# Second output projection: residual rows and two tiles' residuals beside the last attention units, two weight blocks split into the smaller pool

## The chip, the cores and the metric

The kernel runs on one core of a Trainium2 chip. The metric is the device time of one execution in microseconds (us), lower is better; before the change the median of 3 runs is 1395.11 us. Five engines work side by side, each on its own instruction stream, and synchronise by semaphores: TensorE (PE) multiplies matrices, VectorE (DVE), ScalarE (ACT) and GpSimd (POOL) do the elementwise work, and SyncE (SP) issues transfers. Data lies in the on-chip SBUF; matmuls write to PSUM, in banks of 128 partitions by 512 floats.

## The reference

Two encoder layers on 1024 tokens of 1024 channels in float32. Layer A is a dilated sliding-window attention, layer B a latent attention with 16 heads. The change touches only the end of layer B: the output projection `y @ w_out`, and the residual and LayerNorm behind it.

```python
def mixer_mla(u, w_in, q_norm, w_uq, kv_norm, w_ukv, w_out):
    ...
    o = o.transpose(1, 0, 2, 3, 4).reshape(B, S, WIDTH_B)
    y = o * jax.nn.silu(gate)
    return y @ w_out

def reference(...):
    for i in range(DEPTH):
        mod = jax.nn.silu(c) @ ada_w[i] + ada_b[i]
        shift, scale, gate = jnp.split(mod[:, None, :], 3, axis=-1)
        u = x * (1 + scale) + shift
        ...
        x = layernorm(DEEPNORM_ALPHA * x + gate * y, ln_g[i], ln_b[i])
    return x
```

## The kernel before

**Arithmetic.** A float32 product is made of three: each operand is split into a rounded high part and the rest, and high times high, high times low and low times high are added up (`mm3`, lines L89, L90 and L91, one 512-column matmul each). So each weight block and each block of activations needs a high copy (ACT) and a low part, which is source minus high copy (DVE or POOL).

**Attention of layer B** runs over 128 units u, a unit being 128 queries of one head; units stand in pairs w, 64 in all. Four steps of different units are interleaved: scores, softmax, the transposes of the weights (`pth` high and `ptl` low, L1270 to L1274), and for each pair the product with the values (`back(w)`, PE line L1293). `back` ends with `osum`: two copies on ACT (L1298, L1299), a multiply on DVE (L1302), and on POOL a sum (L1305) and the multiply with the gate (L1306) into `gT`, the input of the output projection: 8 blocks of 128 channels. The last pairs, 62 and 63, fill the last tokens of block 7.

**The output projection** works on 8 tiles of 128 tokens, in PSUM tiles `po` of which two exist at a time. Each tile adds up 8 weight blocks times two halves times three products: 48 matmuls. Block b of `wo_b` is loaded (`woraw`, SP), and split by `b_wo_split` into `wh`, `wl` (L101, L102); `b_yt(b, hf)` splits `gT` of block b for one half of the tokens into `ytb` (L1363 on ACT, L1364 on DVE). Half 0 serves tiles 0 to 3, half 1 tiles 4 to 7. Blocks 0 to 3 of tiles 0 and 1 are multiplied beside the last attention units (u = 128 and 129 in the loop), the rest in `layer_b_out`: blocks 4 to 7 of tile 0, then of tile 1, then whole tiles.

**The end of a tile.** The residual tile `x` is loaded from DRAM (L1395) and multiplied by a row and added to another on POOL (L1396, L1397); both rows have been multiplied by ALPHA on ACT (L1390). `finish(i)` multiplies `po` with the gate row (`zb`, L1402), which is the last reader of that PSUM tile; adds the residual (L1403); and after a `yield`, one tile later, does mean, variance and scaling (L1404 to L1410) and stores.

**What sets the order.** PE and SP execute in the order in which the program emits (`manual_schedule(engines=FIXED)`). On DVE, ACT and POOL a scheduler orders the instructions when the program is built. Buffers come from two pools of 128 x 1024 float32 tiles: G with 33 (`gt`) and H with 14 (`ht`); whoever asks for a tile of a full pool waits until an old one has had its last reader.

Of the kernel before, what the change touches and what calls it, by code (L numbers as in the profile page):

```python
# [15 lines left out]
F32 = mybir.dt.float32  # L16
F32R = mybir.dt.float32r
AF = mybir.ActivationFunctionType
ALU = mybir.AluOpType
# [10 lines left out]
ALPHA = math.sqrt(2.0)  # L30
# [11 lines left out]
def f32(ap):  # L42
    return ap.bitcast(F32)
# [23 lines left out]
class Trunk:  # L67
# [1164 lines left out]
    def layer_b_attention(self):  # L1232
        nc = self.nc
        st = {}

        def front(u):
            hd, t = u // 8, u % 8
            q, k = self.q[hd], self.kb[hd % 3]
            s = self.PB.tile([P, 1024], F32, tag="s", bufs=2, name=self.nm("s"))
            ts = slice(t * P, t * P + P)  # L1240
            for j in range(2):
                ks = slice(j * 512, j * 512 + 512)
                self.mm3(s[:, ks], q[0][:, ts], q[1][:, ts], k[0][:, ks], k[1][:, ks], True, True)
            if t == 7:
                self.q.pop(hd)
            st[u] = s

        def soft(u):
            s = st[u]
            m = self.M.tile([P, 4], F32, tag="mb", bufs=4, name=self.nm("mb"))  # L1250
            nc.vector.tensor_reduce(m[:, 0:1], s, axis=AX.X, op=ALU.max, negate=True)  # L1251
            st[u] = (s, m)

        def expo(u):
            s, m = st[u]
            pr = self.ht(F32, "pr")
            nc.scalar.activation(pr, s, AF.Exp, bias=m[:, 0:1], accum_out=m[:, 1:2])  # L1257
            st[u] = (pr, m)

        def middle(u):  # L1260
            pr, m = st.pop(u)
            a = u % 2
            if a == 0:
                st["pt"] = [(self.gt(F32R, "pth"), self.gt(F32R, "ptl")) for _ in range(2)]
                st["den"] = self.M.tile([P, P], F32, tag="den", bufs=3, name=self.nm("den"))
            for j in range(2):
                pt = self.PB.tile([P, 512], F32, tag="t", bufs=4, name=self.nm("t"))
                for c in range(4):
                    kt = 4 * j + c
                    nc.tensor.transpose(pt[:, c * P : c * P + P], pr[:, kt * P : kt * P + P], self.ident)  # L1270
                h, l = (x.rearrange("p (k q) -> p k q", k=4)[:, :, a * P : a * P + P] for x in st["pt"][j])
                src = pt.rearrange("p (k q) -> p k q", k=4)
                nc.scalar.copy(h, src)  # L1273
                nc.vector.tensor_tensor(l, src, f32(h), op=ALU.subtract)  # L1274
            nc.vector.reciprocal(m[:, 2:3], m[:, 1:2])  # L1275
            nc.gpsimd.tensor_copy(st["den"][:, 64 * a : 64 * a + 64], m[:, 2:3].to_broadcast([P, 64]))  # L1276
            if a:
                st[("pv", u // 2)] = (st.pop("pt"), st.pop("den"))

        def back(w):  # L1280
            pts, den = st.pop(("pv", w))
            hd, t0 = w // 4, (w % 4) * 256
            e = hd % 2
            po = self.PB.tile([P, 512], F32, tag="t", bufs=4, name=self.nm("o"))
            nc.tensor.transpose(po[:, 256:384], den, self.ident)
            hq = hd % 4
            n = 0
            for j in range(2):
                for c in range(4):
                    kt = 4 * j + c  # L1290
                    v = self.vq[kt // 2][:, (kt % 2) * 512 + hq * P : (kt % 2) * 512 + hq * P + P]
                    for x in range(2):
                        nc.tensor.matmul(po[:, 0:256], v, pts[j][x][:, c * 256 : c * 256 + 256], start=n == 0, stop=n == 15)  # L1293
                        n += 1
            mine, other = slice(64 * e, 64 * e + 64), slice(64 - 64 * e, 128 - 64 * e)
            g = self.gT[hd // 2][mine, t0 : t0 + 256]
            w3 = self.ht(F32, "osum")
            nc.scalar.copy(w3[mine, 0:256], po[other, 0:256])  # L1298
            nc.scalar.copy(w3[mine, 512:768], po[mine, 0:256])  # L1299
            for a in range(2):  # L1300
                qs = slice(a * P, a * P + P)
                nc.vector.tensor_tensor(  # L1302
                    w3[mine, 256 + a * P : 384 + a * P], po[64 * a : 64 * a + 64, 256:384], g[:, qs], op=ALU.mult
                )
            nc.gpsimd.tensor_tensor(w3[mine, 0:256], w3[mine, 512:768], w3[mine, 0:256], op=ALU.add)  # L1305
            nc.gpsimd.tensor_tensor(g, w3[mine, 0:256], w3[mine, 256:512], op=ALU.mult)  # L1306

        nu = 128
        prep, vprep = iter(()), self.b_v(0)
        self.wo, self.woraw, self.yt, self.po = {}, {}, {}, {}  # L1310
        for u in range(nu + 4):
            p, r = u // 16, u % 16
            if u < nu:
                front(u)
                next(prep, None)
                next(vprep, None)
                soft(u)
            if p + 1 < NPAIR_B:
                if r == 1:
                    self.b_weights(p + 1)  # L1320
                if p % 2 and r == 2:
                    prep = self.b_turn(p + 1)
                if r == 8:
                    prep = self.b_qk(p + 1)
            elif u < nu:
                if r in (1, 3, 5, 7):
                    self.b_wo_load((r - 1) // 2)
                elif r in (4, 6, 8, 10):
                    self.b_wo_split((r - 4) // 2, nc.gpsimd)
                if r in (10, 11, 12, 13):  # L1330
                    self.b_yt(r - 10, 0)
                elif r in (14, 15):
                    for b in (2 * r - 24, 2 * r - 23):
                        self.b_wo_load(b)
            if 0 <= u - 2 < nu:
                middle(u - 2)
                next(vprep, None)
            if u < nu:
                expo(u)
            if u == nu:  # L1340
                self.b_out_blocks(0, range(4))
            if u == nu + 1:
                self.b_out_blocks(1, range(4))
            if u >= 4 and u % 2 == 0 and u < nu + 4:
                back((u - 4) // 2)
            if u % 32 == 2 and 32 < u < nu:
                vprep = self.b_v(u // 32)
            next(vprep, None)
            next(prep, None)

    def b_wo_load(self, b):
        raw = self.woraw[b] = self.ht(F32, "woraw")
        self.nc.sync.dma_start(raw, self.A["wo_b"][b])

    def b_wo_split(self, b, lo_engine):
        self.wo[b] = self.w_split(self.woraw.pop(b), lo_engine=lo_engine)

    def b_yt(self, b, hf):

# [22 lines left out]
    def layer_b_out(self):  # L1382
        nc = self.nc
        for b in range(4, 8):
            self.b_wo_split(b, nc.gpsimd if b == 6 else nc.vector)
            self.b_yt(b, 0)
        rg, rb, lng, lnb = (self.ln_row(i) for i in range(4))
        gate = self.ada_row(1)
        for t in (rg, rb):
            nc.scalar.mul(t, t, ALPHA)  # L1390
        xs = {}

        def x1(i):
            t = xs[i] = self.ht(F32, "x1")
            nc.sync.dma_start(t, self.xn_d[i])  # L1395
            nc.gpsimd.tensor_tensor(t, t, rg, op=ALU.mult)  # L1396
            nc.gpsimd.tensor_tensor(t, t, rb, op=ALU.add)  # L1397

        def finish(i):
            z, x = self.ht(F32, "zb"), xs.pop(i)  # L1400
# [12 lines left out]
        def last(i):  # L1413
# [22 lines left out]
            for ns in HALVES:  # L1436
                nc.vector.scalar_tensor_tensor(w[:, ns], w[:, ns], mv[:, 7:8], lnb[:, ns], op0=ALU.mult, op1=ALU.add)
                nc.sync.dma_start(self.out[i * P : i * P + P, ns], w[:, ns])

        x1(0)  # L1440
        active = iter(())
        for i in range(7):
            self.b_out_blocks(i, range(4 if i < 2 else 0, 8))
            if i in (1, 2):
                for b in range(4 * i - 4, 4 * i):
                    self.b_yt(b, 1)
            x1(i + 1)
            for _ in active:
                pass
            active = finish(i)  # L1450
            next(active)
        for _ in active:
            pass
        last(7)
# [85 lines left out]
```

## Time and profile before

| | |
|---|---|
| Median of 3 runs | 1395.11 us (1394.83 to 1395.6) |
| Profiled execution, own time | 1399.57 us |
| Profiled execution, span from first to last instruction | 1397.8 us |
| Granted TensorE clock, mean of the span | 0.993 |
| PE busy | 1355.3 us, 97% |
| DVE busy | 938.9 us, 67% |
| ACT busy | 820.3 us, 59% |
| POOL busy | 573.6 us, 41% |

The profiled execution is one single run with the profiler on. All places below are given in its own clock, from the first instruction on; the change's stretch lies at 1283 to 1340 us. The name behind a line number is that of the output and the inputs, without buffer numbers. A figure in brackets is the time for which the engine had nothing to do before, with what ended it.

### The profile page before, as it was taken

What the parts mean: (1) busy time and instruction counts of PE and PEld (TensorE: products, weight loads), DVE (VectorE), ACT (ScalarE), POOL (GpSimd) and SP (SyncE); (2) the same over time, 40 slices, a digit from 0 to 9 for tenths busy, and PEclk for the clock granted to TensorE, in tenths of its full rate; (3) what the DMA queues carried; (4) which work ended last, traced back from release to release, by engine and by line L of the source; (5) the groups of instructions that cost most, each with busy time, mean ns of one, the idle gap of its engine ahead of it and who ended that gap; (6) DMA issues with size and microseconds to landing.
All of it is one profiled execution on the core that took longest, in us unless ns stands there. A gap on an engine that the chain in (4) does not pass through costs nothing.

```text
span 1397.8 us, 21019 instructions
## 1 busy us (share of the span) xinstructions
PE 1355.3 (97%) x7523; PEld 1160.8 (83%) x7523; DVE 938.9 (67%) x1708; ACT 820.3 (59%) x1604; POOL 573.6 (41%) x657
## 2 busy tenths in 40 slices
PE   6999999999999999999999999999999999999897
PEld 5788888888888788888987888888889888898786
DVE  7654354555455492746745178898988889888787
ACT  3575565565443452425752178788787878888321
POOL 5341233132122226903742254634463463444653
PEclk9999999999999999999999999999999999999999
DMA  9422211022244302544145001010010100014132
GB/s 356 112 64 36 59 50 50 25 60 73 95 151 123 99 31 77 180 149 151 61 119 166 21 14 37 16 30 16 22 29 18 35 16 16 16 61 133 49 113 83
DMA packets 39721, 105.26 MB, mean 75 GB/s; under 512 B 5126, under 2 KB 11270, under 8 KB 39617
## 3 DMA queue, kind: packets, MB, share of 16 engines
q1 hardware_dynamic: 35608, 91.80, 21.3%
q0 software_dynamic: 3552, 12.06, 3.5%
q8 instruction: 60, 0.98, 0.3%
q14 instruction: 45, 0.36, 0.1%
q10 hardware_dynamic: 456, 0.05, 0.0%
HBM read 87.60 MB, written 8.43 MB: 69 GB/s over the span
## 4 chain that ended last, share of the span: by engine, by line
PE 74%; DVE 12%; ACT 5%; issue 4%; DMA 4%; SPq 0%; POOL 0%; DVEq 0%; ACTq 0%
PE pj L89 7%; PE pj L91 7%; PE pj L90 7%; PE o L1293 5%; PE t L1270 5%; PE po L89 4%; PE po L91 4%; PE po L90 4%; DVE mb L1251 3%; PE s L91 3%; PE s L89 3%; PE s L90 3%; PE pg L89 2%; PE pg L90 2%; PE pg L91 2%
## 5 line engine op out<-in xcount | busy, mean ns | idle before, releaser
L89 PE MATMUL pj<-uh,wh 128*128 128x512 f32 x528 | 216.0, 409 | 0.0
L91 PE MATMUL pj<-uh,wl 128*128 128x512 f32 x528 | 207.4, 393 | 0.0
L90 PE MATMUL pj<-ul,wh 128*128 128x512 f32 x528 | 207.4, 393 | 0.0
L1274 DVE TENSOR_TENSOR ptl<-t,pth 128x512 fp32r<-128x512 f32 x256 | 165.4, 682 | 3.0 <-ACT pth L1273 0.9
L1251 DVE TENSOR_REDUCE mb<-s 128x1 f32<-128x1024 f32 x128 | 155.8, 1217 | 7.9 <-PE s L91 6.3
L1257 ACT ACTIVATE pr<-s,mb 128x1024 f32<-128x1024 f32 x128 | 143.4, 1120 | 29.2 <-DVE mb L1251 21.1
L1273 ACT CAST pth<-t 128x512 fp32r<-128x512 f32 x256 | 138.9, 589 | 36.2 <-PE t L1270 34.1
L102 POOL TENSOR_TENSOR wl<-wraw,wh 128x1024 fp32r<-128x1024 f32 x43 | 106.6, 2485 | 106.7 <-ACT wh L101 54.6
L1270 PEld LDWEIGHTS t<-ident,pr 128*128 128x128 f32 x1024 | 119.3, 140 | 19.7 <-DVE ptl L1274 2.6
L1270 PE MATMUL t<-ident,pr 128*128 128x128 f32 x1024 | 133.2, 272 | 1.9 <-DVE ptl L1274 1.9
L1293 PE MATMUL o<-pth,vq 128*128 128x256 f32 x512 | 130.4, 292 | 0.0
L1293 PE MATMUL o<-ptl,vq 128*128 128x256 f32 x512 | 125.5, 283 | 0.8 <-DVE ptl L1274 0.8
L507 ACT ACTIVATE sb<-sb,stat 128x256 f32<-128x256 f32 (+1 forms) x144 | 67.0, 467 | 98.6 <-DVE stat L501 98.5
L91 PEld LDWEIGHTS pj<-uh,wl 128*128 128x128 f32 x528 | 99.4, 188 | 22.2
L1276 POOL COPY den<-mb 128x64 f32<-128x64 f32 x128 | 30.1, 236 | 203.2 <-DVE mb L1275 193.6
L90 PEld LDWEIGHTS pj<-ul,wh 128*128 128x128 f32 x528 | 100.1, 190 | 14.3
L89 PEld LDWEIGHTS pj<-uh,wh 128*128 128x128 f32 x528 | 99.9, 189 | 14.5
L89 PE MATMUL s<-kb,q 128*128 128x512 f32 x256 | 104.4, 408 | 0.2 <-ACT pr L1257 0.2
L91 PE MATMUL s<-kb,q 128*128 128x512 f32 x256 | 101.3, 396 | 0.0
L90 PE MATMUL s<-kb,q 128*128 128x512 f32 x256 | 100.8, 394 | 0.0
L1293 PEld LDWEIGHTS o<-ptl,vq 128*128 128x128 f32 x512 | 97.7, 191 | 1.4 <-DVE ptl L1274 1.4
L1293 PEld LDWEIGHTS o<-pth,vq 128*128 128x128 f32 x512 | 97.7, 191 | 0.2
(288 smaller groups left out, 3317.6 us busy)
## 6 DMA issues: line engine op xcount, KB each, us to landing
wraw<-wa SPq DMA_DIRECT2D x36, 512.0 KB, 4.9
ada<-ada_row SPq DMA_DIRECT2D x64, 256.0 KB, 3.6
wraw<-wo_a SPq DMA_DIRECT2D x18, 512.0 KB, 3.6
ada<-ada_ss SPq DMA_DIRECT2D x16, 512.0 KB, 8.2
kb<-kb POOLq DMA_DIRECT2D x30, 256.0 KB, 3.4
xc<-xt SPq DMA_DIRECT2D x8, 512.0 KB, 9.2
xr<-x SPq DMA_DIRECT2D x8, 512.0 KB, 5.7
xn_d<-z POOLq DMA_DIRECT2D x8, 512.0 KB, 4.6
```

The lines of the kernel that those rows point to most:

```text
L89: mm(out, wh, xh, start=start, stop=False)
L90: mm(out, wh, xl, start=False, stop=False)
L91: mm(out, wl, xh, start=False, stop=stop)
L102: (lo_engine or self.nc.gpsimd).tensor_tensor(l[:, :width], raw[:, :width], f32(h[:, :width]), op=ALU.subtract)
L507: nc.scalar.activation(sb[:, a * w : a * w + w], sb[:, a * w : a * w + w], AF.Exp, bias=stat[:, 0, hh, t : t + 1], scale=-1.0, accum_out=s ...
L1251: nc.vector.tensor_reduce(m[:, 0:1], s, axis=AX.X, op=ALU.max, negate=True)
L1257: nc.scalar.activation(pr, s, AF.Exp, bias=m[:, 0:1], accum_out=m[:, 1:2])
L1270: nc.tensor.transpose(pt[:, c * P : c * P + P], pr[:, kt * P : kt * P + P], self.ident)
L1273: nc.scalar.copy(h, src)
L1274: nc.vector.tensor_tensor(l, src, f32(h), op=ALU.subtract)
L1276: nc.gpsimd.tensor_copy(st["den"][:, 64 * a : 64 * a + 64], m[:, 2:3].to_broadcast([P, 64]))
L1293: nc.tensor.matmul(po[:, 0:256], v, pts[j][x][:, c * 256 : c * 256 + 256], start=n == 0, stop=n == 15)
```

## The change

The two rows of the residual are loaded and scaled at u = 128 (`b_residual_rows`), and the residuals of tiles 0 and 1 are prepared there and at u = 129 (`b_residual`), ahead of those tiles' first four blocks; later tiles' residuals are asked for two tiles ahead, behind `finish`. `b_wo_split` takes the split blocks 6 and 7 from pool H instead of G, and makes the high copy with `copy` instead of `activation`. The half-1 `b_yt` of four blocks each stand behind the first part of `finish` of tiles 1 and 2, not ahead of it. The gate row is loaded ahead of the two late LayerNorm rows.

```diff
             if u == nu:
+                self.b_residual_rows()
+                self.b_residual(0)
                 self.b_out_blocks(0, range(4))
             if u == nu + 1:
+                self.b_residual(1)
                 self.b_out_blocks(1, range(4))
...
+    def b_residual_rows(self):
+        self.rows = self.ln_row(0), self.ln_row(1)
+        for t in self.rows:
+            self.nc.scalar.mul(t, t, ALPHA)
+        self.xs = {}
+
+    def b_residual(self, i):
+
+        nc = self.nc
+        t = self.xs[i] = self.ht(F32, "x1")
+        nc.sync.dma_start(t, self.xn_d[i])
+        nc.gpsimd.tensor_tensor(t, t, self.rows[0], op=ALU.mult)
+        nc.gpsimd.tensor_tensor(t, t, self.rows[1], op=ALU.add)
...
     def b_wo_split(self, b, lo_engine):
-        self.wo[b] = self.w_split(self.woraw.pop(b), lo_engine=lo_engine)
+        raw = self.woraw.pop(b)
+        h, l = self.wo[b] = [(self.ht if b >= 6 else self.gt)(F32R, x) for x in ("woh", "wol")]
+        self.nc.scalar.copy(h, raw)
+        lo_engine.tensor_tensor(l, raw, f32(h), op=ALU.subtract)
...
-        rg, rb, lng, lnb = (self.ln_row(i) for i in range(4))
         gate = self.ada_row(1)
-        for t in (rg, rb):
-            nc.scalar.mul(t, t, ALPHA)
-        xs = {}
-
-        def x1(i):
-            t = xs[i] = self.ht(F32, "x1")
-            nc.sync.dma_start(t, self.xn_d[i])
-            nc.gpsimd.tensor_tensor(t, t, rg, op=ALU.mult)
-            nc.gpsimd.tensor_tensor(t, t, rb, op=ALU.add)
+        lng, lnb = self.ln_row(2), self.ln_row(3)
+        xs = self.xs
...
-        x1(0)
         active = iter(())
         for i in range(7):
             self.b_out_blocks(i, range(4 if i < 2 else 0, 8))
-            if i in (1, 2):
-                for b in range(4 * i - 4, 4 * i):
-                    self.b_yt(b, 1)
-            x1(i + 1)
             for _ in active:
                 pass
             active = finish(i)
             next(active)
+            if i in (1, 2):
+                for b in range(4 * i - 4, 4 * i):
+                    self.b_yt(b, 1)
+            if i < 6:
+                self.b_residual(i + 2)
```

The order that the build makes of it differs on the three scheduled engines. In the change's program the split is L1375 and L1376 (`woh`, `wol`), the `ytb` L1383 and L1384, the row scaling L1357, the residual passes L1365 and L1366, and `zb` L1414.

On DVE, where blocks 5 to 7 are split and tile 0 is closed, before the change; `gT_6555`, `gT_6612` and `gT_6643` are blocks 5, 6 and 7, and the `ytb` from `gT_6171` on (blocks 0, 1, ...) are those of half 1:

```order
L1364 TENSOR_TENSOR ytb_12983<-gT_6555,ytb_12983 128x512
L1302 TENSOR_TENSOR osum_12965<-o_12947,gT_6643 64x128 x2
L1364 TENSOR_TENSOR ytb_12990<-gT_6612,ytb_12990 128x512
L102 TENSOR_TENSOR wl_12994<-woraw_12815,wh_12993 128x1024
L1364 TENSOR_TENSOR ytb_12997<-gT_6643,ytb_12997 128x512
L1364 TENSOR_TENSOR ytb_13073<-gT_6171,ytb_13073 128x512
L1364 TENSOR_TENSOR ytb_13076<-gT_6249,ytb_13076 128x512
L1364 TENSOR_TENSOR ytb_13079<-gT_6316,ytb_13079 128x512
L1402 TENSOR_TENSOR zb_13044<-po_12856,row_13008 128x1024
L1364 TENSOR_TENSOR ytb_13082<-gT_6407,ytb_13082 128x512
L1402 TENSOR_TENSOR zb_13095<-po_12922,row_13008 128x1024
L1364 TENSOR_TENSOR ytb_13149<-gT_6484,ytb_13149 128x512
```

And of the change, from the half-0 `ytb` of block 7 on:

```order
L1384 TENSOR_TENSOR ytb_13011<-gT_6643,ytb_13011 128x512
L1384 TENSOR_TENSOR ytb_13088<-gT_6171,ytb_13088 128x512
L1384 TENSOR_TENSOR ytb_13091<-gT_6249,ytb_13091 128x512
L1384 TENSOR_TENSOR ytb_13094<-gT_6316,ytb_13094 128x512
L1302 TENSOR_TENSOR osum_12979<-o_12961,gT_6643 64x128 x2
L1384 TENSOR_TENSOR ytb_13097<-gT_6407,ytb_13097 128x512
L1384 TENSOR_TENSOR ytb_13164<-gT_6484,ytb_13164 128x512
L1384 TENSOR_TENSOR ytb_13167<-gT_6555,ytb_13167 128x512
L1384 TENSOR_TENSOR ytb_13170<-gT_6612,ytb_13170 128x512
L1376 TENSOR_TENSOR wol_13008<-woraw_12815,woh_13007 128x1024
L1384 TENSOR_TENSOR ytb_13173<-gT_6643,ytb_13173 128x512
L1414 TENSOR_TENSOR zb_13044<-po_12866,row_13014 128x1024
```

The low part of block 7 (`wl_12994` before, `wol_13008` now) stood ahead of every half-1 `ytb`, and stands behind seven of them now; `zb_13044` stands behind all eight, and no longer between them.

On ACT, from the `ytb` of block 5 on (`woraw_12813` and `woraw_12815` are the raw blocks 6 and 7), before the change:

```order
L1363 ACTIVATE ytb_12983<-gT_6555 128x512
L101 ACTIVATE wh_12986<-woraw_12813 128x1024
L1298 COPY osum_12965<-o_12947 64x256
L1299 COPY osum_12965<-o_12947 64x256
L1363 ACTIVATE ytb_12990<-gT_6612 128x512
L101 ACTIVATE wh_12993<-woraw_12815 128x1024
L1363 ACTIVATE ytb_12997<-gT_6643 128x512
L1363 ACTIVATE ytb_13073<-gT_6171 128x512
L1390 ACTIVATE lnrow_13000<-lnrow_13000 128x1024
L1390 ACTIVATE lnrow_13002<-lnrow_13002 128x1024
```

And of the change, where the scaled rows stand further up, right behind the high copy of block 4:

```order
L1383 ACTIVATE ytb_12997<-gT_6555 128x512
L1383 ACTIVATE ytb_13004<-gT_6612 128x512
L1383 ACTIVATE ytb_13011<-gT_6643 128x512
L1383 ACTIVATE ytb_13088<-gT_6171 128x512
L1383 ACTIVATE ytb_13091<-gT_6249 128x512
L1383 ACTIVATE ytb_13094<-gT_6316 128x512
L1298 COPY osum_12979<-o_12961 64x256
L1299 COPY osum_12979<-o_12961 64x256
L1375 CAST woh_13000<-woraw_12813 128x1024
L1383 ACTIVATE ytb_13097<-gT_6407 128x512
L1383 ACTIVATE ytb_13164<-gT_6484 128x512
L1383 ACTIVATE ytb_13167<-gT_6555 128x512
```

The high copy of block 6 stood behind one `ytb` and stands behind six now, and that of block 7 follows four further ones, two rows below the last shown.

On POOL, from the last attention unit's `den` on (`osum_12899` before and `osum_12909` of the change are pair 62, `osum_12965` and `osum_12979` pair 63), before the change:

```order
L1276 COPY den_12839<-mb_12811 128x64
L1305 TENSOR_TENSOR osum_12899<-osum_12899 64x256
L1306 TENSOR_TENSOR gT_6643<-osum_12899 64x256
L102 TENSOR_TENSOR wl_12987<-woraw_12813,wh_12986 128x1024
L1305 TENSOR_TENSOR osum_12965<-osum_12965 64x256
L1306 TENSOR_TENSOR gT_6643<-osum_12965 64x256
L1396 TENSOR_TENSOR x_2244_13012<-x_2244_13012,lnrow_13000 128x1024
L1396 TENSOR_TENSOR x_2245_13040<-x_2245_13040,lnrow_13000 128x1024
```

And of the change:

```order
L1276 COPY den_12839<-mb_12811 128x64
L1365 TENSOR_TENSOR x_2221_12862<-x_2221_12862,lnrow_12856 128x1024
L1366 TENSOR_TENSOR x_2221_12862<-x_2221_12862,lnrow_12858 128x1024
L1305 TENSOR_TENSOR osum_12909<-osum_12909 64x256
L1365 TENSOR_TENSOR x_2227_12932<-x_2227_12932,lnrow_12856 128x1024
L1306 TENSOR_TENSOR gT_6643<-osum_12909 64x256
L1366 TENSOR_TENSOR x_2227_12932<-x_2227_12932,lnrow_12858 128x1024
L1305 TENSOR_TENSOR osum_12979<-osum_12979 64x256
L1376 TENSOR_TENSOR wol_13001<-woraw_12813,woh_13000 128x1024
L1306 TENSOR_TENSOR gT_6643<-osum_12979 64x256
```

The passes over the residuals of tiles 0 and 1 stood behind everything else, and now stand ahead of and between the sums of pairs 62 and 63, with the low part of block 6 behind them.

On SP the two scaled rows are followed by the residuals of tiles 0 and 1, then by the gate row and the two late rows; before, all four rows and the gate row came first.

## Rows read from the trace of the kernel before

**Rows 1.** Page: busy time by engine, and one group of attention work.
```profile
PE 1355.3 (97%) x7523; PEld 1160.8 (83%) x7523; DVE 938.9 (67%) x1708; ACT 820.3 (59%) x1604; POOL 573.6 (41%) x657
...
L1273 ACT CAST pth<-t 128x512 fp32r<-128x512 f32 x256 | 138.9, 589 | 36.2 <-PE t L1270 34.1
```

**Rows 2.** Timeline, PE: start us, us, engine, line, operation, [idle before, releaser].
```profile
1303.24 0.28 PE L1293 MATMUL o<-ptl,vq 128*128 128x256 f32 x1
...
1305.03 0.40 PE L89 MATMUL po<-wh,ytb 128*128 128x512 f32 x1
...
1313.06 0.39 PE L89 MATMUL po<-wh,ytb 128*128 128x512 f32 x1
...
1317.59 0.39 PE L91 MATMUL po<-wh,ytb 128*128 128x512 f32 x1
1320.97 0.80 PE L89 MATMUL po<-wh,ytb 128*128 128x512 f32 x1 [2.99 <-DVE zb L1402]
```

**Rows 3.** Windows: us, busy of the engines, PEclk, DMA share, GB/s.
```profile
477.00:482.00 5.00, 4.94 (x20) 4.19 (x20) 0.42 (x1) 2.87 (x4) 0.00 (x0) 0.66 0.00 0
1321.00:1327.00 6.00, 6.00 (x14) 4.74 (x15) 5.30 (x4) 1.26 (x2) 6.00 (x3) 0.50 0.00 0
```

**Rows 4.** Timeline, DVE, output projection; columns as in group 2.
```profile
1295.82 1.23 DVE L102 TENSOR_TENSOR wl<-woraw,wh 128x1024 fp32r<-128x1024 f32 x1 [3.92 <-PE o L1293]
...
1299.05 0.59 DVE L1302 TENSOR_TENSOR osum<-o,gT 64x128 f32<-64x128 f32 x2
1299.68 1.29 DVE L1274 TENSOR_TENSOR ptl<-t,pth 128x512 fp32r<-128x512 f32 x2
...
1308.38 1.75 DVE L102 TENSOR_TENSOR wl<-woraw,wh 128x1024 fp32r<-128x1024 f32 x1
...
1314.78 2.10 DVE L1364 TENSOR_TENSOR ytb<-gT,ytb 128x512 fp32r<-128x512 f32 x1 [0.70 <-ACT ytb L1363]
...
1319.69 1.22 DVE L1402 TENSOR_TENSOR zb<-po,row 128x1024 f32<-128x1024 f32 x1
...
1328.70 0.69 DVE L1364 TENSOR_TENSOR ytb<-gT,ytb 128x512 fp32r<-128x512 f32 x1 [0.70 <-ACT ytb L1363]
```

**Rows 5.** Timeline, POOL, same stretch and after it.
```profile
1298.70 0.94 POOL L1305 TENSOR_TENSOR osum<-osum 64x256 f32<-64x256 f32 x1 [7.04 <-ACT osum L1299]
...
1305.51 2.41 POOL L102 TENSOR_TENSOR wl<-woraw,wh 128x1024 fp32r<-128x1024 f32 x1 [4.98 <-ACT wh L101]
...
1310.82 5.52 POOL L1396 TENSOR_TENSOR x<-x,lnrow 128x1024 f32<-128x1024 f32 x2
...
1349.51 2.45 POOL L1396 TENSOR_TENSOR x<-x,lnrow 128x1024 f32<-128x1024 f32 x1 [2.28 <-DMA x<-xn_d]
```

**Rows 6.** Timeline, ACT, same stretch.
```profile
1291.03 1.10 ACT L101 ACTIVATE wh<-woraw 128x1024 fp32r<-128x1024 f32 x1
1295.88 0.63 ACT L1363 ACTIVATE ytb<-gT 128x512 fp32r<-128x512 f32 x1 [3.75 <-PE o L1293]
...
1303.79 0.63 ACT L1363 ACTIVATE ytb<-gT 128x512 fp32r<-128x512 f32 x1 [4.14 <-PE o L1293]
...
1305.40 0.36 ACT L1298 COPY osum<-o 64x256 f32<-64x256 f32 x1
...
1307.65 1.14 ACT L1363 ACTIVATE ytb<-gT 128x512 fp32r<-128x512 f32 x2
...
1316.92 0.64 ACT L1363 ACTIVATE ytb<-gT 128x512 fp32r<-128x512 f32 x1 [2.17 <-DVE ytb L1364]
```

**Rows 7.** Timeline, SP: the four row transfers and the first residual tiles.
```profile
1283.86 4.30 SPq L781 DMA_DIRECT2D lnrow<-ln  x4
...
1289.11 0.85 SPq L1395 DMA_DIRECT2D x<-xn_d  x2
```

**Rows 8.** DMA issues, 1240 to 1330: KB each, median us to landing.
```profile
x<-xn_d SPq DMA_DIRECT2D x3, 512.0 KB, 5.5
```

**Rows 9.** Timeline, PE, layer A: the other stretch with a low clock.
```profile
476.72 0.74 PE L518 MATMUL t<-ident,sb 128*128 128x128 f32 x2 [2.07 <-ACT sb L507]
```

## Prediction

> **What bounds the kernel now.** The page comes first: TensorE (PE) is busy 97% of the span [rows 1], so only PE's idle time and its clock are left to win or lose. The PE timeline of the change's stretch comes next [rows 2]. One 512-column matmul takes (1317.59 − 1313.06) / 20 = 0.2265 us. Tile 0's blocks 4 to 7 begin at 1305.03; the last matmul of tile 1 starts at 1317.59, and then PE is idle 2.99 us until tile 2 at 1320.97, released by `zb_0` on VectorE (DVE): tile 2 needs the PSUM pair that `zb_0` frees. The windows [rows 3] show what follows: granted clock 0.50 (1.2 of 2.4 GHz) from 1321 to 1327, in which (1 − 0.50) × 6.00 = 3.0 us of PE's work is lost. So the place costs about 6 us. Why is `zb_0` late? The DVE timeline [rows 4] has it at 1319.69, behind two-input `ytb` subtractions of the half that only tile 4 needs. Each waits for ScalarE (ACT), which waits for the `ytb` before (2.17 us idle) [rows 6], and each takes 2.1 us instead of the 0.69 of one alone [rows 4].
>
> The POOL timeline says why they are slow. The first two residual passes end at 1310.82 + 5.52 = 1316.34 [rows 5], and the `ytb` that began at 1314.78 ends at 1316.88 [rows 4], 0.54 us later: it did nothing until the passes were over. So I read it as waiting for the whole POOL instruction; `zb`, which reads PSUM, took its 1.22 in the same stretch, so I let only DVE operations with two SBUF inputs wait. The Trainium skill says the same in "SBUF — State Buffer", section "SBUF: two separate sides": VectorE with two SBUF inputs and GpSimd take their shared port pair for a whole instruction, whichever starts first, and the other blocks. If they shared by halves instead, the wait at `wol_4` below would be about 1.2 us and not 2.2, and the sum 1 us smaller; the row's 0.54 bears the rule out.
>
> **The change, part by part.** All times are in the trace's clock.
>
> (a) *Moved transfers.* On the SP queue, tile residuals 0 and 1 take the places of the third and fourth LayerNorm row, which left within 1283.86 to 1288.16; at 5.5 us each they land by about 1293.7 [rows 7, 8], while before they left only from 1289.11. The gate and the two late rows are wanted only after 1319. Cost 0; if they came 1 us late, the POOL passes below would shift by that.
>
> (b) *Row scaling on ACT.* Two of the size that took 1.10 [rows 6] now stand behind `woh_4` (ends 1292.13), to 1294.3, inside ACT's idle 3.75 us before 1295.88 [rows 6]. Cost 0; without that cover it would be 2.2.
>
> (c) *The passes of tiles 0 and 1 move ahead of POOL's gate sums*, and so beside DVE's `wol_4`, `ytb_4`, `wol_5`. One pass alone took 2.45 [rows 5]. Tile 0's run 1293.2 to 1295.65 and to 1298.1. `wol_4`, wanted at 1295.82 [rows 4], finds the second pass in progress by 0.2 us and ends 1.1 behind it, at 1299.2 instead of 1297.0. The gate sum of unit pair 62 follows (its 0.94 [rows 5] held a DVE wait; 0.6 without), to 1299.8, `ytb_4` to 1300.35, tile 1's first pass to 1302.8, `wol_5` to 1303.9 instead of 1299.05, two `osum` (0.59) to 1304.5, the first `ptl` (0.65) to 1305.15 [rows 4]. PE wants that `ptl` at 1303.24 [rows 2]: 1.9 us late. The listed durations overlap their neighbours by about 0.1 (1295.82 + 1.23 is past the next start), so I take 1.6; bounds 0.1 (DVE first at `wol_4`) and 1.9. This is a new PE stall.
>
> (d) *Blocks 6 and 7.* Blocks 4 and 5 are 12 matmuls and now end at 1305.03 + 1.6 + 2.72 = 1309.35. On ACT `ytb_5`, which a matmul of pair 63 lets go (1303.79 before [rows 6]), slips to 1305.4. The four buffers that blocks 6 and 7 leave free in pool G let six `ytb` go at once, and the build puts them ahead of `woh_6`: 6 × 0.57 + 0.73 (two copies) + 1.10 gives 1310.6 [rows 6], less 0.2 of overlap 1310.4: stall 1.0. `wol_6` on POOL takes 2.41 more [rows 5], to 1312.9; PE, after one matmul, wants it at 1310.6: stall 2.3. Six matmuls bring PE to 1314.3, where it wants `wol_7`. On DVE the `ytb` caught by `wol_6` ends at 1313.45, `osum` at 1314.0, four `ytb` of the late half at 0.6 at 1316.4, one of them held 0.6 by the gate multiply of pair 63 (1317.0), `wol_7` 1.15: 1318.2. Stall 3.9. Before, `wol_7` began at 1308.38 [rows 4], ahead of all late `ytb`. Bounds of its end: 1317.45 (DVE first at `wol_4`, which carries through) and 1318.8 (every hand-over 0.1 longer).
>
> The hi copy as CAST instead of ACTIVATE: at half the size 0.59 in the mean of the attention's casts [rows 1] against 0.63 for an ACTIVATE [rows 6], so 0, at most 0.1 per block. Pool H is full here; what waits for its buffers in the new order is SP (the gate row, the late rows and tile 2's residual, all wanted after 1319), not the splits of blocks 6 and 7. So 0 for that.
>
> (e) *Tile 2.* From `wol_7` 29 matmuls are left: 29 × 0.2265 = 6.57, and tile 2 starts at 1324.8 instead of 1320.97: **+3.8**. `zb_0` no longer holds it: tile 0's last matmul is over by 1319.6, `zb_0` needs 1.22, behind at most one `ytb`, about 1321.5. So the 2.99 us is gone but sits inside the new stalls, 1.6 + 1.0 + 2.3 + 3.9 = 8.8.
>
> (f) *Clock.* The clock fell to half after an idle of 2.99 [rows 2, 3], and earlier after one of 2.07 at 476.72 [rows 9], with (1 − 0.66) × 5.00 = 1.7 us lost within 477 to 482 [rows 3]. An idle of 3.9 behind 2.3 should do it too: 1.7 to 3.0 lost instead of 3.0, and I take 2.6: **−0.4**.
>
> (g) *Later tiles and tail.* From 1327 PE ran without a break; each tile's DVE work has 10.9 us to hide behind (48 matmuls). `zb_1`, now behind `zb_0`'s first steps, is due near 1329 and wanted by tile 3 near 1335.7. The tail behind the last matmul is not touched. Cost 0; if DVE fell behind, up to 2 us per tile.
>
> Sum: +3.8 − 0.4 = **+3.4**. The profiled execution took 1399.57 us, 4.46 above the median of the runs, 1395.11; I carry the difference over: 1395.1 + 3.4 = 1398.5.
>
> **Rivals.**
> 1. *Likeliest: the port waits push `wol_6` and `wol_7` late*, as above: 1398.5, own range 1397.9 to 1399.5. Chance 0.44.
> 2. *DVE gets the port first at `wol_4`* (a tie of 0.2 us), `wol_7` ends at 1317.45, tile 2 starts at 1324.0, +3.05, and the half clock is the short one of 477, −1.3: +1.7, 1396.8. Nothing speaks against it but the order of two starts. Chance 0.26.
> 3. *No DVE operation of this stretch waits for POOL* (faster). Then `woh_6` is there at 1309.0, `wol_6` at 1311.4, `wol_7` at about 1313.4, tile 2 starts at 1320.0 (−1.0), and if those shorter stalls leave the clock up, −3.0 more: −4.0, 1391.1. It decides where `wol_7` ends before 1314.6 and the clock stays at 1.0. Against it: the 2.1 us of [rows 4]. Chance 0.12.
> 4. *The clock falls twice*, first behind the stalls of block 6 (1.0 + 2.3 with one matmul between): the next six matmuls at half speed lose 1.3, and the stretch after `wol_7` 3.0: +3.8 + 1.3 and, with a late hand-over, about +5.2, 1400.3. Chance 0.18.
>
> **How the numbers follow.** 0.2% is 2.8 us, about what a measurement here tells from no change. Faster is case 3, 0.12; same is case 2, 0.26; slower are 1 and 4, 0.62. The range leaves out case 3 and the far end of case 4: 1393.5 to 1401.5. The time is that of case 1.
>
> **What would show it.** In the changed profile: a PE idle of 1 to 2 us before a `ptl` matmul near 1303; idles before block 6's first and second matmul, the second released by POOL; a longer one near 1314 to 1318 released by DVE's `wol`; no idle before tile 2; half clock for 3 to 6 us around 1318 to 1325; DVE's `wol_4` and `wol_5` at over 2 us each. It is wrong if `wol_4` stays at 1.23, if the chip lets `wol_7` go before 1315, or if PE idles in a later tile.

## The result and the profile after

The change made the kernel slower: 1399.65 us median of 6 runs (1398.71 to 1401.1) against 1395.16 of 6 runs of the kernel before; the ratio is 1.0036, 95% interval 1.0025 to 1.0047, so +3.5 to +6.6 us.

The profiled execution of the changed kernel took 1399.06 us, with a span of 1397.3, half a us *less* than the one of before. The two spans can't be set against each other as they stand: the row of windows of each kernel over the same 20 us of layer A shows a granted clock of 0.91 before and of 1.00 after, in a stretch that the change does not touch (and 0.99 against 1.00 over the first 200 us). Of before (PEclk is the third figure from the end):

```profile
470.00:490.00 20.00, 17.70 (x111) 14.35 (x110) 9.91 (x24) 9.62 (x18) 5.04 (x4) 0.91 0.26 81
```

And of after:

```profile
470.00:490.00 20.00, 17.71 (x116) 14.29 (x115) 11.89 (x21) 11.53 (x16) 5.04 (x4) 1.00 0.20 63
```

So I count from one instruction that both have: DVE's `wol_4` (before: `wl_4`) starts at 1295.82 [rows 4] and at 1291.79, 4.03 us earlier. From there to the end of the span it is 1397.8 − 1295.82 = 101.98 before and 1397.3 − 1291.79 = 105.51 after: **+3.5**, in the stretch that was changed. To place a time of after beside one of before, 4.03 is added.

PE's busy line of the page, to be read with [rows 1]:

```profile
PE 1353.7 (97%) x7523; PEld 1160.4 (83%) x7523; DVE 934.8 (67%) x1708; ACT 819.3 (59%) x1604; POOL 571.5 (41%) x657
```

The PE timeline of after, from the last attention pair to tile 2, with three rows from behind it. It answers to [rows 2]: every bracket is an idle PE.

```profile
1300.97 0.39 PE L1293 MATMUL o<-ptl,vq 128*128 128x256 f32 x1 [1.60 <-DVE ptl L1274]
...
1306.76 0.49 PE L89 MATMUL po<-woh,ytb 128*128 128x512 f32 x1 [0.98 <-ACT woh L1375]
1309.31 0.80 PE L90 MATMUL po<-wol,ytb 128*128 128x512 f32 x1 [2.05 <-POOL wol L1376]
...
1311.61 0.63 PE L89 MATMUL po<-woh,ytb 128*128 128x512 f32 x1
1314.67 0.50 PE L90 MATMUL po<-wol,ytb 128*128 128x512 f32 x1 [2.43 <-DVE wol L1376]
...
1315.94 0.54 PE L89 MATMUL po<-woh,ytb 128*128 128x512 f32 x1
...
1319.59 0.39 PE L89 MATMUL po<-woh,ytb 128*128 128x512 f32 x1
...
1323.06 0.39 PE L89 MATMUL po<-woh,ytb 128*128 128x512 f32 x1
...
1331.22 0.40 PE L89 MATMUL po<-woh,ytb 128*128 128x512 f32 x1
...
1334.02 0.39 PE L89 MATMUL po<-woh,ytb 128*128 128x512 f32 x1
...
1388.96 0.28 PE L91 MATMUL po<-woh,ytb 128*128 128x256 f32 x1
```

There are four stalls, before the first `ptl` and in blocks 6 and 7 of tile 0, 1.60 + 0.98 + 2.05 + 2.43 = 7.06 us. Tile 2's first matmul (1323.06) carries no bracket: the 2.99 us wait for `zb` is gone. The DVE and POOL timelines show whom the stalls wait for, beside [rows 4] and [rows 5]; a row with x6 is six instructions in one run.

```profile
1291.79 3.29 DVE L1376 TENSOR_TENSOR wol<-woraw,woh 128x1024 fp32r<-128x1024 f32 x1 [3.92 <-PE o L1293]
...
1296.16 3.42 DVE L1376 TENSOR_TENSOR wol<-woraw,woh 128x1024 fp32r<-128x1024 f32 x1
...
1302.30 7.51 DVE L1384 TENSOR_TENSOR ytb<-gT,ytb 128x512 fp32r<-128x512 f32 x6 [0.79 <-ACT ytb L1383]
...
1310.44 3.03 DVE L1384 TENSOR_TENSOR ytb<-gT,ytb 128x512 fp32r<-128x512 f32 x4
1313.40 1.21 DVE L1376 TENSOR_TENSOR wol<-woraw,woh 128x1024 fp32r<-128x1024 f32 x1
...
1316.14 1.23 DVE L1414 TENSOR_TENSOR zb<-po,row 128x1024 f32<-128x1024 f32 x1 [0.93 <-PE po L91]
```

The POOL timeline of after, same stretch:

```profile
1291.61 2.39 POOL L1366 TENSOR_TENSOR x<-x,lnrow 128x1024 f32<-128x1024 f32 x1
...
1295.76 2.73 POOL L1365 TENSOR_TENSOR x<-x,lnrow 128x1024 f32<-128x1024 f32 x1
...
1306.84 2.41 POOL L1376 TENSOR_TENSOR wol<-woraw,woh 128x1024 fp32r<-128x1024 f32 x1 [0.35 <-POOL osum L1305]
```

`wol_4` began at 1291.79, 0.18 us behind the pass that ran from 1291.61 to 1294.00, and ended 1.08 us behind that pass: 3.29 us for an operation of 1.23. `wol_5` met the next pass (1295.76 to 1298.49) and took 3.42. Block 7's low part is the row at 1313.40, behind the ten `ytb` of the two rows above it, seven of them of the late half; before, that operation stood at 1308.38 [rows 4], ahead of that half. The ACT timeline shows the same order, beside [rows 6]:

```profile
1301.63 3.24 ACT L1383 ACTIVATE ytb<-gT 128x512 fp32r<-128x512 f32 x6 [6.03 <-PE o L1293]
...
1305.67 1.04 ACT L1375 CAST woh<-woraw 128x1024 fp32r<-128x1024 f32 x1
1306.62 2.19 ACT L1383 ACTIVATE ytb<-gT 128x512 fp32r<-128x512 f32 x4
1308.71 1.03 ACT L1375 CAST woh<-woraw 128x1024 fp32r<-128x1024 f32 x1
```

Six `ytb`, two copies, then the high copy of block 6 at 1305.67; four more `ytb`, then that of block 7. The windows of after show the clock, beside [rows 3]:

```profile
1306.00:1310.00 4.00, 1.19 (x3) 0.78 (x4) 3.99 (x3) 3.74 (x6) 2.91 (x2) 0.90 0.00 0
1310.00:1314.00 4.00, 2.24 (x6) 1.23 (x4) 3.96 (x7) 0.63 (x1) 1.17 (x1) 0.67 0.27 90
1314.00:1318.00 4.00, 3.33 (x11) 2.63 (x12) 3.04 (x4) 0.00 (x0) 2.69 (x2) 0.75 0.10 41
```

It fell twice: behind the 2.05 us idle (the five steps from 1309.31 to 1311.61 took 2.30 us instead of 1.13, so some 1.4 more for the six matmuls) and again at 1315.94, until 1319.59 (nine matmuls in 3.65 us, 1.6 more).

The later tiles have no idle, but they are a little slower. From tile 2 to the last matmul PE takes 1388.96 − 1323.06 = 65.90 us, and took 1389.48 − 1320.97 = 68.51 before. That is 2.6 less, although before lost 3.0 there at half clock [rows 3]; so 0.4 is lost elsewhere. It lies in blocks 6 and 7: their twelve matmuls in tile 2 take 1334.02 − 1331.22 = 2.80 us, and took 1334.89 − 1332.17 = 2.72. The PE timeline of before has these rows:

```profile
1332.17 0.39 PE L89 MATMUL po<-wh,ytb 128*128 128x512 f32 x1
...
1334.89 0.39 PE L89 MATMUL po<-wh,ytb 128*128 128x512 f32 x1
...
1389.48 0.28 PE L91 MATMUL po<-wh,ytb 128*128 128x256 f32 x1
```

### The profile page after: what moved, and what is told of

It reads as the page before. It is cut to its first block, busy times and chain, and to the rows that moved or that the text cites. A ratio compares the mean times of both kernels' runs of the same rounds, so it can differ in the third digit from the quotient of the medians.

```text
span 1397.3 us, 21017 instructions
## 1 busy us (share of the span) xinstructions
PE 1353.7 (97%) x7523; PEld 1160.4 (83%) x7523; DVE 934.8 (67%) x1708; ACT 819.3 (59%) x1604; POOL 571.5 (41%) x657
## 4 chain that ended last, share of the span: by engine, by line
PE 75%; DVE 13%; ACT 5%; issue 4%; DMA 3%; SPq 0%; DVEq 0%; ACTq 0%
PE pj L89 7%; PE pj L90 7%; PE pj L91 7%; PE o L1293 5%; PE t L1270 5%; PE po L90 4%; PE po L91 4%; PE po L89 4%; DVE mb L1251 3%; PE s L91 3%; PE s L89 3%; PE s L90 3%; PE pg L89 2%; PE pg L91 2%; PE pg L90 2%
```

## The experiments

All are compared with runs of the kernel before on the same chip (medians 1394.54 for the first four, 1394.29 for the last three). The change had its own runs of before (1395.16), so a version is set beside the change by its distance from its own runs of before; the distance of the change is +4.5 us. Three theories were to be told apart. **Theory 1**: two separate losses, the early residual passes hold DVE on the shared port, and the pool split lets the late `ytb` go ahead of blocks 6 and 7. **Theory 2**: the passes alone. **Theory 3**: the later tiles.

**Blocks 6 and 7 split into pool G again**, the rest as in the change.

```diff
-        h, l = self.wo[b] = [(self.ht if b >= 6 else self.gt)(F32R, x) for x in ("woh", "wol")]
+        h, l = self.wo[b] = [self.gt(F32R, x) for x in ("woh", "wol")]
```

> The change with the split blocks 6 and 7 taken from pool G again; all else stays (early rows and residuals, CAST, order of the late ytb). Theory 1 (two causes: the pool split lets the late ytb go ahead of the splits of blocks 6 and 7, 4 to 5 us of stalls; the early residual passes cost one stall of 1.6 us by the shared port, and save the wait for zb_0): the high copies of 6 and 7 stand ahead of the late ytb again, the stalls in blocks 6 and 7 sum to about 2.3 us instead of 5.5, the one before the first ptl stays at 1.6, no idle over 0.6 before tile 2, and with the clock up at least from there about 1391.5 us (1390 to 1395). Theory 2 (the residual passes beside DVE's work make all of the loss, the pool is harmless): 1398 us or more. Theory 3 (the later tiles lose, by the residuals asked two tiles ahead): 1398 or more, with idle PE behind 1340.

Measured: 1391.62 us, ratio 0.9982 (0.9974 to 0.9991): 2.9 us faster than before, where the change is 4.5 slower. Its PE timeline:

```profile
1301.79 0.39 PE L1293 MATMUL o<-ptl,vq 128*128 128x256 f32 x1 [1.58 <-DVE ptl L1274]
...
1307.23 0.50 PE L90 MATMUL po<-wol,ytb 128*128 128x512 f32 x1 [0.41 <-POOL wol L1376]
...
1309.45 0.49 PE L90 MATMUL po<-wol,ytb 128*128 128x512 f32 x1 [0.24 <-DVE wol L1376]
1310.59 0.50 PE L91 MATMUL po<-woh,ytb 128*128 128x512 f32 x1 [0.64 <-DVE ytb L1384]
...
1317.45 0.50 PE L89 MATMUL po<-woh,ytb 128*128 128x512 f32 x1 [0.21 <-DVE zb L1414]
```

The first stall is the change's (1.58); those in blocks 6 and 7 are 0.41 + 0.24 + 0.64 instead of 5.46, and the clock stayed at 1.00 from 1300 to the last matmul. In its DVE timeline the low part of block 7 stands behind the `ytb` of blocks 5 and 6 and ahead of the late half, as before:

```profile
1307.65 1.75 DVE L1376 TENSOR_TENSOR wol<-woraw,woh 128x1024 fp32r<-128x1024 f32 x1
```

Theory 2 and theory 3 fall: the same passes and the same later residuals cost nothing on balance once the splits stand in front of the late `ytb`.

**The pool split alone**, on the kernel before (with the change's `copy` for the high part).

```diff
-        self.wo[b] = self.w_split(self.woraw.pop(b), lo_engine=lo_engine)
+        raw = self.woraw.pop(b)
+        h, l = self.wo[b] = [(self.ht if b >= 6 else self.gt)(F32R, x) for x in ("woh", "wol")]
+        self.nc.scalar.copy(h, raw)
+        lo_engine.tensor_tensor(l, raw, f32(h), op=ALU.subtract)
```

> The kernel before, with only the split of blocks 6 and 7 (high copy by copy, both parts in pool H); rows, residuals and ytb stay where they were. Theory 1: three stalls in blocks 6 and 7 of about 1.0, 2.2 and 1.3 to 2.5 us come, the 2.99 before tile 2 goes, the half clock stays: 1396.0 to 1398.5 us. Theory 2: no stall in blocks 6 and 7 beyond those of before, time within 1 us of before (1394 to 1396).

Measured: 1394.77 us, ratio 0.9999 (0.9990 to 1.0008). The time is the one that I had put down for theory 2, the profile is theory 1's. Its PE timeline:

```profile
1305.07 0.50 PE L89 MATMUL po<-woh,ytb 128*128 128x512 f32 x1 [0.99 <-ACT woh L1358]
1307.57 0.50 PE L90 MATMUL po<-wol,ytb 128*128 128x512 f32 x1 [2.00 <-POOL wol L1359]
...
1311.61 0.50 PE L90 MATMUL po<-wol,ytb 128*128 128x512 f32 x1 [2.37 <-DVE wol L1359]
```

And its window in which the clock was low:

```profile
1312.00:1316.00 4.00, 4.00 (x12) 3.15 (x11) 3.58 (x2) 0.00 (x0) 4.00 (x2) 0.58 0.00 0
```

All three stalls are there, 5.36 us in sum, and no idle before tile 2 (2.99 before). What I had too high is the clock: (1 − 0.58) × 4.00 = 1.7 us lost where the kernel before loses 3.0 [rows 3]. More stall and less half clock cancel. So the split is not free without the early passes; it trades one loss for another.

**Rows and residuals two units earlier**, all splits in pool G.

```diff
+            if u == nu + -2:
+                self.b_residual_rows()
+            if u == nu + -2:
+                self.b_residual(0)
+            if u == nu + -1:
+                self.b_residual(1)
             if u == nu:
-                self.b_residual_rows()
-                self.b_residual(0)
                 self.b_out_blocks(0, range(4))
             if u == nu + 1:
-                self.b_residual(1)
                 self.b_out_blocks(1, range(4))
...
-        h, l = self.wo[b] = [(self.ht if b >= 6 else self.gt)(F32R, x) for x in ("woh", "wol")]
+        h, l = self.wo[b] = [self.gt(F32R, x) for x in ("woh", "wol")]
```

> The change with all splits in pool G and with the rows and tile 0's residual asked at u = 126 and tile 1's at u = 127, so that their POOL passes are over before DVE splits blocks 4 and 5. Theory 1: no stall before the first ptl, two of 0.6 and 0.9 in block 7, none before tile 2, clock at 1.0 throughout the projection: 6 us less than before, about 1389 us (1387.5 to 1391). Theory 2 (early passes cost wherever they stand beside DVE): 1395 or more.

Measured: 1388.59 us, ratio 0.9956 (0.9942 to 0.9969). This version beats both kernels: it is 6 us below before, and the change is 4.5 above. DVE's `wol_4` in its DVE timeline:

```profile
1290.57 2.76 DVE L1379 TENSOR_TENSOR wol<-woraw,woh 128x1024 fp32r<-128x1024 f32 x1 [2.03 <-PE o L1293]
```

And all idle of PE between 1270 and the end, in its PE timeline:

```profile
1304.93 0.49 PE L90 MATMUL po<-wol,ytb 128*128 128x512 f32 x1 [0.25 <-DVE wol L1379]
1306.07 0.50 PE L91 MATMUL po<-woh,ytb 128*128 128x512 f32 x1 [0.65 <-DVE ytb L1387]
```

No stall at a `ptl`, none before tile 2, clock 1.00. It did not go quite as I wrote, that all passes would be over: tile 1's first pass still meets `wol_4`, which takes 2.76 us, and its second starts at 1294.61, beside `wol_5`, and itself takes 3.26 us in the POOL timeline. But only one pass is left in DVE's way, tile 0's two being through, and that much DVE has in hand before PE wants the `ptl`.

**The same with the pool split of the change.** The edit is the last one without its second part, so that the pool line is that of the change.

> The same with the rows and residuals at u = 126 and 127, but blocks 6 and 7 split into pool H as in the change. Theory 1: the stalls of blocks 6 and 7 of 1.0, 2.2 and 1.3 to 2.5 us are all that is left, and bring the half clock: 4 to 7 us above the run with all splits in pool G, 1393 to 1396.5 us. Theory 2: no slower than that run by more than 1 us.

Measured: 1394.87 us, ratio 1.0000 (0.9989 to 1.0011), 6.3 us above the run without the split. Its PE timeline:

```profile
1307.65 0.50 PE L89 MATMUL po<-woh,ytb 128*128 128x512 f32 x1 [0.99 <-ACT woh L1378]
1310.14 0.79 PE L90 MATMUL po<-wol,ytb 128*128 128x512 f32 x1 [1.99 <-POOL wol L1379]
...
1314.17 0.50 PE L90 MATMUL po<-wol,ytb 128*128 128x512 f32 x1 [1.11 <-DVE wol L1379]
```

The split's stalls come back with the same releasers, 0.99 + 1.99 + 1.11, and five matmuls at half clock from 1310.14 on, while no `ptl` is late. So they are the split's own.

**The passes of tiles 0 and 1 left out**, all else the change, the pool split too.

```diff
         t = self.xs[i] = self.ht(F32, "x1")
         nc.sync.dma_start(t, self.xn_d[i])
+        if i < 2:
+            return
```

> The change with the POOL passes over the residuals of tiles 0 and 1 left out (those two tiles' outputs lack the scaled residual), all else as in the change, the pool split too. Theory 1 (DVE's splits of blocks 4 and 5 wait for those passes on the shared port, and blocks 6 and 7 for the order of the build): wol_4 at 1.23 us instead of 3.29, no idle before the first ptl, but still about 1.0, 2.0 and 1.2 to 2.4 us in blocks 6 and 7; time 1.6 to 4 us below the change, 1395.5 to 1398. Theory 2 (the passes make all of it): the idles in blocks 6 and 7 go too, 1391 or less.

Measured: 1394.32 us, ratio 1.0001 (0.9992 to 1.0011), level with before and so 4.5 us below the change (5.3 by the bare medians), more than the 1.6 to 4 expected. `wol_4` in its DVE timeline:

```profile
1290.58 1.23 DVE L1378 TENSOR_TENSOR wol<-woraw,woh 128x1024 fp32r<-128x1024 f32 x1 [3.92 <-PE o L1293]
```

And the stalls in its PE timeline:

```profile
1303.69 0.50 PE L89 MATMUL po<-woh,ytb 128*128 128x512 f32 x1 [0.99 <-ACT woh L1377]
1306.18 0.79 PE L90 MATMUL po<-wol,ytb 128*128 128x512 f32 x1 [2.00 <-POOL wol L1378]
...
1310.21 0.50 PE L90 MATMUL po<-wol,ytb 128*128 128x512 f32 x1 [1.10 <-DVE wol L1378]
```

`wol_4` is back at 1.23 us and the stall at the `ptl` is gone: these two are the passes' doing. The 4.5 is made of the 1.60 of that stall, 1.33 in block 7 (1.10 instead of 2.43) and the second half-clock stretch, 1.6, which does not come. The 1.33 is the passes' doing too: without them DVE is through the six `ytb` (3.70 us instead of 7.51) and the two `osum` at 1303.53, before POOL's `wol_6` starts at 1303.76; in the change the `osum` stand behind `wol_6`, at 1309.82.

**Each pass in two halves.** This asks how DVE waits for POOL.

```diff
-        nc.gpsimd.tensor_tensor(t, t, self.rows[0], op=ALU.mult)
-        nc.gpsimd.tensor_tensor(t, t, self.rows[1], op=ALU.add)
+        for r, op in zip(self.rows, (ALU.mult, ALU.add)):
+            for ns in HALVES if i < 2 else (slice(0, 1024),):
+                nc.gpsimd.tensor_tensor(t[:, ns], t[:, ns], r[:, ns], op=op)
```

> The change with each POOL pass of tiles 0 and 1 made as two of 512 columns; the work is the same. If DVE waits for a whole POOL instruction, it gets in between two halves: wol_4 takes about 1.0 us less than 3.29, the idle before the first ptl shrinks from 1.6 to under 0.5, and part of it comes back in block 6, whose low part POOL starts later; the time is within 2 us of the change. If the two share the port by bandwidth, or if the passes hold DVE by their total, wol_4 stays near 3.29 and the idle at 1.6.

Measured: 1397.66 us, ratio 1.0032 (1.0020 to 1.0043), +3.4 us on before. `wol_4` and `wol_5` in its DVE timeline:

```profile
1289.61 2.21 DVE L1377 TENSOR_TENSOR wol<-woraw,woh 128x1024 fp32r<-128x1024 f32 x1 [3.92 <-PE o L1293]
...
1293.46 1.76 DVE L1377 TENSOR_TENSOR wol<-woraw,woh 128x1024 fp32r<-128x1024 f32 x1
```

And the later stalls in its PE timeline:

```profile
1305.79 0.57 PE L90 MATMUL po<-wol,ytb 128*128 128x512 f32 x1 [2.58 <-POOL wol L1377]
...
1311.75 0.79 PE L90 MATMUL po<-wol,ytb 128*128 128x512 f32 x1 [3.01 <-DVE wol L1377]
```

`wol_4` took 2.21 us instead of 3.29, one half pass less, and the `ptl` came in time. The same POOL work in shorter instructions holds DVE for less, so DVE waits for the instruction in progress, not for a share of the port. The Trainium skill's page "SBUF — State Buffer", section "SBUF: two separate sides", states such a lock for the whole instruction; this run agrees. Most of the gain went again: POOL, held by DVE between its halves, and DVE behind it were later for blocks 6 and 7 (2.58 and 3.01 instead of 2.05 and 2.43).

**PE's idle filled.** 27 matmuls that nobody reads stand in front of the three products of blocks 6 and 7 that wait.

```diff
+                if i == 0 and b >= 6 and ns.start == 0:
+                    self.filled(b, ps, y[:, ts], y[:, tl], h[:, ns], l[:, ns], b == 7)
+                    continue
...
+    def filled(self, b, out, wh, wl, xh, xl, stop):
+        mm = self.nc.tensor.matmul
...
+        def fill(n):
+            for _ in range(n):
+                mm(self.idle, self.yt[0, 0][:, 0:P], self.wo[0][0][:, 0:512], start=True, stop=True)
+
+        fill(4 if b == 6 else 0)
+        mm(out, wh, xh, start=False, stop=False)
+        fill(9 if b == 6 else 14)
+        mm(out, wh, xl, start=False, stop=False)
+        mm(out, wl, xh, start=False, stop=stop)
```

> The change with 27 matmuls into an unused bank, that nobody reads, in the three places where PE waits in blocks 6 and 7 of tile 0: 4 before the first product of block 6, 9 before its second, 14 before block 7's second (0.9, 2.0 and 3.2 us at full clock, each under its wait). If the half clock comes from the idle, the clock stays at 1.0 through the projection, wol_7 ends where it did, and the 1.6 us that the second half-clock stretch costs behind it go: 1398.0 us (1397 to 1399). If the clock doesn't depend on that idle, it falls as before and the time is 1399.6 or more.

Measured: 1397.12 us, ratio 1.0020 (1.0011 to 1.0029), +2.8 us on before instead of +4.5, for more work. PE's only idle behind the `ptl` stall, in its PE timeline:

```profile
1312.18 0.50 PE L1417 MATMUL po<-wol,ytb 128*128 128x512 f32 x1 [0.53 <-DVE wol L1376]
```

And the clock, in one window over blocks 4 to 7:

```profile
1302.00:1320.00 18.00, 17.34 (x74) 13.26 (x73) 15.65 (x20) 8.55 (x14) 10.11 (x5) 1.00 0.09 30
```

The clock is 1.00 all through. So the half clock of the change comes from these idles, and what it costs beside the idle itself is 1.6 us by the rows of after. The medians give 1.7, but the intervals of the two ratios overlap (1.0011 to 1.0029 and 1.0025 to 1.0047), so the time alone would not show it.

## Why the prediction was right

The forecast was 1398.5, +3.4 us; measured were 1399.65 and +4.5, and +3.5 by the profile from `wol_4` on. The +3.5 is the lower end of the measured interval; the 1.0 us between the two is not placed. The chain that was forecast is the one in the profile. That the sum agrees within 0.1 is luck in part, for four misses cancel in it.

- *Passes beside DVE's splits, step (c)*: forecast a second pass in progress by 0.2 us and a stall of 1.6; it was 0.18 and 1.60. Shown by the runs without and with halved passes.
- *Blocks 6 and 7, step (d)*: forecast 1.0, 2.3 and 3.9; it was 0.98, 2.05 and 2.43. `wol_7` ended at 1313.40 + 1.21 + 4.03 = 1318.64 in the clock of before, forecast 1318.2, so the chain was right; the third stall is smaller because PE came to it late, at half clock.
- *Clock, step (f)*: mis-sized. I had one stretch with 2.6 us lost behind `wol_7`. There were two: the first lost 1.4 that lay under the wait for `wol_7` and cost nothing, the second 1.6. The 3.0 that the kernel before loses was right.
- *Tile 2, step (e)*: no idle, as forecast. Its start, 1323.06 + 4.03 = 1327.09, is the 1318.64 of `wol_7` plus 6.57 of matmuls plus the 1.6 of the clock, within 0.3.
- *Later tiles, step (g)*: put at 0, and 0.4 by the rows of tile 2 to the last matmul. PE shows no idle behind 1314.67 in after, and DVE did not fall behind; but the matmuls of blocks 6 and 7 are slower, a term that the prediction does not have.
- *The sum*: the parts were off by −1.0 (the stretch behind `wol_7`), +0.4 (`wol_7` later than forecast), +0.3 (tile 2's start) and +0.4 (later tiles), which makes +3.5 of the +3.4.
- *The rivals*: DVE was not first at `wol_4` (2). DVE did wait for POOL (3). The clock did fall twice (4), but its first fall lay inside a wait, so that rival's price of 1.3 for it was wrong.

What the prediction did not see is how the two losses stand to each other: I had put the passes and the pool split into one chain. Taken apart, the change without the split gains 2.9 us on the kernel before, the change without the passes beside `wol_4` is level with it, and only both together lose. The rows say why. The kernel before loses some 6 us ahead of and in tile 2 (2.99 idle, 3.0 at half clock), and either part takes most of that away by itself: the idle ahead of tile 2 is 0.21 without the split and none with the split alone. Together they save it once, and pay for both.

## What to carry to other kernels

Before work is moved to an idle engine, look at which instruction of the neighbour meets it, and for how long: here an off-path POOL pass of 2.4 us in front of a 1.2 us DVE operation on the critical chain cost its whole remainder. More room in a pool is not only room: freed buffers let less urgent work become ready, and the build may then put it ahead of what the bottleneck waits for, as it did here; read the built order, not only the program. Two changes that cure the same wait gain it once, so each is to be measured with and without the other. And a gain from an early start needs the start to be early enough: two units made 1391.6 into 1388.6.

## What the hardware showed that I had not expected

The clock did not fall at the restart behind the 2.43 us idle: five matmuls ran at full speed, from 1314.67 to 1315.94, and the nine behind them took 3.65 us. In the run with the splits in pool G, idles of 1.58, 0.41, 0.24 and 0.64 within 9 us brought no fall. The length of the low stretch also differed: 6 us at 0.50 behind one idle of 2.99 [rows 2, 3], 1.7 us lost behind 2.37 in the run with the split alone. And idles of 0.99 and 2.00 in a row were followed by full speed in the run with the split alone (its row of 1307.57: the first matmul took 0.50), and by half clock in the run without passes (0.79 in the row of 1306.18). So the lengths of the idles alone do not give the price. What sets it was not tried.

The matmuls of blocks 6 and 7 have another pace with their weights in pool H. In tiles 3 to 6 one takes 0.232 to 0.233 us from start to start, and one of blocks 1 to 5 takes 0.227. All six profiles with the pool split show it, and none of the three with these blocks in pool G, two of which make the high part by `copy` too. Why the place of a weight should matter was not tried.

Also, the profiles differ by some 2 us in layer A, which is the same program in all, according to whether the clock falls near 477 us. It fell (0.91 in the window from 470 to 490) in that of before, of the run with the splits in G and of the one with early rows and the split, and not (1.00) in the others.
